# Fourteen expert tiles loaded into the ring before and beside the query weights, and priority for the choice of experts

## The chip, the cores and the metric

The kernel runs on one core of a Trainium2 chip. A core has five engines that run side by side and meet at semaphores: TensorE (PE in the profile), VectorE (DVE), ScalarE (ACT), GpSimd (POOL) and SyncE (SP). Sixteen DMA engines move data between HBM and the core's memory; here SP issues the plain loads and POOL issues the gathers of single rows. The metric is device time in microseconds (us) of one execution, the median of several.

## What is computed

One decoder block on 256 tokens of width 1024, all in float32: a state-space mixer beside causal attention, a gated merge, then an expert layer and a gated embedding. The change lies in the expert layer:

```python
def peer_ffn(h, w_q, keys1, keys2, u_tab, v_tab):
    q = (h @ w_q).reshape(B, S, 8, 2, 128)
    s1 = einsum('bshd,hnd->bshn', q[..., 0, :], keys1)   # 8 heads x 128 scores
    s2 = einsum('bshd,hnd->bshn', q[..., 1, :], keys2)
    v1, i1 = top_k(s1, 16);  v2, i2 = top_k(s2, 16)
    top, flat = top_k(v1[:, None] + v2[None, :], 16)     # 16 of 16 x 16 sums
    experts = e1 * 128 + e2                              # of 16,384 experts
    act = gelu(einsum('td,thkd->thk', h, u_tab[experts]))
    return einsum('thk,thkd->td', softmax(top) * act, v_tab[experts])
```

## The kernel before, in words

The kernel has two phases. Phase 1 (mixer, attention, merge) streams its weights in pieces of 512 KB through nine slots of a pool, `stream`; its pieces are asked for seven ahead of their use, `pssm` and `wout` among the last. The query weights `wq` come after them through the same slots. Phase 2 is the expert layer.

**The two halves of the tokens are treated differently.** For the first 128 tokens the products with *all* 16,384 experts are computed: the table `u` is read as 128 tiles of 512 KB, four tiles make a group (`s_group(g)`, 16 matmuls into `sp`, line 786), and the table `v` follows as 128 tiles. For the second 128 tokens only the chosen rows are fetched: `dot_rows(j)` gathers 128 rows of `u` (one row for each of 128 tokens) by an indirect DMA (line 750) and forms the dot products on VectorE (line 796); `v_chosen` does the like for `v`.

**The ring.** All of these tiles, `u` and `v` tiles (`dn`, issued by SP at line 745) and gathered rows (`sel`, issued by POOL), share one ring of `RING = 14` slots of 512 KB. A slot is given out in the order in which the program asks for it: the 15th asker waits until the first one's reader is done. Before the change the program asks in the order of use, four `u` tiles of a group, then two or three rows, then four `u` tiles:

```python
for g in range(GRP // 2):
    s_group(g)
    rows_until(g)          # rows up to (g + 1) * 88 // 32
    if g < 8:
        for i in (2 * g, 2 * g + 1):
            best(0, i, sc0[:, i, :])
    elif g < 10:
        choose(0, g - 8)
    elif g == 10:
        turn_choices(0)
```

**What must come before the rows.** The scores are made list by list: `lists(i)`, 16 of them, takes the piece `wq[i]`, splits it in two (ScalarE at line 116, POOL at line 120), multiplies (lines 144 to 147), turns the result into scores (line 840), copies them (lines 842 and 843; the copy `sc1` of the second half of the tokens has three buffers) and lets VectorE pick the 16 best (`best`, lines 824 to 828). After lists 0 to 7 `choose(1, 0)` combines them, on VectorE, into the row numbers `rowU` of the first 64 gathers (line 914); after lists 8 to 15 `choose(1, 1)` does the rest. `choose(0, 0)` and `choose(0, 1)` do the same later for the first 128 tokens, and `turn_choices(0)` then transposes their result on TensorE (line 929).

**What sets the order.** A scheduler in the compiler orders each engine's instructions ahead of time: of those that its own timing takes to be ready, it issues the one that the program names first, and a block under `tc.high_priority()` ranks ahead of the rest. Each engine then runs its list in that order. Matmuls under `in_turn()` stay in the order in which they are written.

Of the kernel before, what the change touches and what calls it, by code (L numbers as in the profile page):

```python
# [60 lines left out]
NS_POOL = 9  # L61
PLAN2 = "abr0c1d23"
RING = 14
GRP = NE // 4
DOTS_BY = 40
ROWS_FROM = 46
# [14 lines left out]
def block_kernel(ctx, tc, xT_d, xn_d, small_d, pos_d, pT_d, w_in_d, glu_d, pssm_d, patt_d, wout_d, wq_d,  # L81
# [32 lines left out]
    def split(src, hi, lo, pool_cols=None):  # L114

        nc.scalar.activation(hi, src, AF.Copy)  # L116
        n = src.shape[-1]
        pc = n if pool_cols is None else pool_cols
        if pc > 0:
            nc.gpsimd.tensor_tensor(lo[:, :pc], src[:, :pc], hi.bitcast(F32)[:, :pc], ALU.subtract)  # L120
        if pc < n:
            nc.vector.tensor_tensor(lo[:, pc:], src[:, pc:], hi.bitcast(F32)[:, pc:], ALU.subtract)

    def fetch(src_d):
        nat = stream.tile([P, PW], F32, name="nat", tag="w", bufs=WBUFS)
        nc.sync.dma_start(nat, src_d)
        return nat

    def piece(src_d, pool_cols=None, nat=None, at=None):
        if nat is None:  # L130
            nat = fetch(src_d)
        if at is None:
            hi = stream.tile([P, PW], F32R, name="whi", tag="w", bufs=WBUFS)
            lo = stream.tile([P, PW], F32R, name="wlo", tag="w", bufs=WBUFS)
        else:
            hi, lo = at
        split(nat, hi, lo, lo_cols[0] if pool_cols is None else pool_cols)
        return hi, lo

    def mm3(ps, pairs):  # L140

        n = len(pairs)
        for i, ((lh, ll), (rh, rl)) in enumerate(pairs):
            nc.tensor.matmul(ps, lh, rh, start=(i == 0), stop=False)  # L144
            nc.tensor.matmul(ps, lh, rl, start=False, stop=False)  # L145
        for i, ((lh, ll), (rh, rl)) in enumerate(pairs):
            nc.tensor.matmul(ps, ll, rh, start=False, stop=(i == n - 1))
# [96 lines left out]
    with ExitStack() as p1:  # L244
# [22 lines left out]
        def take():  # L267
            while len(ahead) < LEAD + 1 and todo:
                cut()
            return ahead.pop(0)  # L270
# [20 lines left out]
        w = D // SEG  # L291
# [344 lines left out]
        with tc.manual_schedule(engines={mybir.EngineType.PE}):  # L636
            for n, x in enumerate("u" * 4 + "q" * 4 + "k" * 4 + "v" * 4 + "z" * 16 + TAIL):
                while steps and steps[0][0] <= n:
                    steps.pop(0)[1]()
                i = counts.get(x, 0)  # L640
                counts[x] = i + 1
                pc = take()
# [13 lines left out]
        for i in range(4):  # L656
            pc = take()
# [7 lines left out]
        for c in range(DC):  # L665
            pc = take()
# [76 lines left out]
    def fetch_dense(src_d):  # L743
        nat = dense.tile([P, PW], F32, name="dn", tag="ring", bufs=RING)
        nc.sync.dma_start(nat, src_d)
        return nat

    def fetch_rows(src_d, rows):
        sel = dense.tile([P, D], F32, name="sel", tag="ring", bufs=RING)
        nc.gpsimd.indirect_dma_start(out=sel, out_offset=None, in_=src_d,  # L750
                                     in_offset=bass.IndirectOffsetOnAxis(ap=rows, axis=0))
        return sel
# [3 lines left out]
    def in_turn():  # L756
        return tc.issue_after(pe[0].ins) if pe[0] is not None else ExitStack()
# [7 lines left out]
        nc.scalar.activation(h1n[:, h * 512:(h + 1) * 512], ps, AF.Copy)  # L765

    turned_s = []

    def s_turn():

        g, sn = turned_s.pop(0)
        pt = psS.tile([P, 512], F32, name="pt", tag="T")
        with in_turn():
            for q in range(4):
                pe[0] = nc.tensor.transpose(pt[:, q * P:(q + 1) * P], sn[:, q * P:(q + 1) * P], ident)
        nc.scalar.activation(s_slots(g), pt.rearrange("p (q t) -> p q t", q=4), AF.Copy)

    def s_group(g):

        ps = psS.tile([P, 512], F32, name="sp", tag="S")  # L780
        for i in range(4):
            w = fetch_dense(u_d[4 * g + i]).rearrange("p (k n) -> p k n", k=2)
            with in_turn():
                for k in range(2):
                    c = 2 * i + k
                    pe[0] = nc.tensor.matmul(ps, hn[:, c, :P], w[:, k, :], start=(c == 0), stop=(c == DC - 1))  # L786
        sn = hx.tile([P, 512], F32, name="sn", bufs=2)
        nc.scalar.activation(sn, ps, AF.Gelu_apprx_tanh)  # L788
        if turned_s:
            s_turn()  # L790
        turned_s.append((g, sn))

    def dot_rows(j):

        sel = fetch_rows(urow_d, rowU[:, j:j + 1])
        nc.vector.scalar_tensor_tensor(sel, sel, 1.0, h1n, ALU.mult, ALU.mult, accum_out=dots[:, j:j + 1])  # L796

    with tc.tile_pool(name="topk", bufs=1, reuse_waits="tile") as tk:
# [21 lines left out]
        def best(t, i, sc):  # L820

            v1, ix = v1s[t], ixs[t]
            s2 = tk.tile([P, P], F32, name="s2", bufs=2)
            nc.vector.max(v1[:, i, 0:8], sc)
            nc.vector.match_replace(s2, v1[:, i, 0:8], sc, -3.0e38)
            nc.vector.max(v1[:, i, 8:16], s2)
            nc.vector.max_index(ix[:, i, 0:8], v1[:, i, 0:8], sc)
            nc.vector.max_index(ix[:, i, 8:16], v1[:, i, 8:16], s2)

        def lists(i):  # L830
            pc = piece(wq_d[i])
            ps = psS.tile([P, 512], F32, name="q2p", tag="S")
            with in_turn():
                hi, lo = (z.rearrange("p (k n) -> p k n", k=8) for z in pc)
                mm3(ps[:, :T], [((hi[:, k], lo[:, k]), (h2[0][:, k], h2[1][:, k])) for k in range(8)])
            q2 = tk.tile([P, T], F32, name="q2", bufs=2)
            nc.scalar.activation(q2, ps[:, :T], AF.Copy)
            px = psX.tile([P, 512], F32, name="scp", tag="X")
            for t in (1, 0):
                nc.tensor.matmul(px[:, t * P:(t + 1) * P], q2[:, t * P:(t + 1) * P], keys[:, i, :], start=True, stop=True)  # L840
            sc1 = tk.tile([P, P], F32, name="sc1", bufs=3)
            nc.scalar.activation(sc1, px[:, P:T], AF.Copy)
            nc.scalar.activation(sc0[:, i, :], px[:, :P], AF.Copy)
            best(1, i, sc1)
# [97 lines left out]
        for half in range(2):  # L942
            for i in range(8 * half, 8 * half + 8):
                lists(i)
            choose(1, half)
        nsel = 0

        def rows_until(g):
            nonlocal nsel
            while nsel < (g + 1) * (P - DOTS_BY) // GRP:  # L950
                dot_rows(nsel)
                nsel += 1

        for g in range(GRP // 2):
            s_group(g)
            rows_until(g)
# [7 lines that stand above are left out]
            elif g == 11:  # L964
                turn_choices(1)
# [59 lines left out]
    done = 0  # L1025
    for g in range(GRP // 2, GRP):
        s_group(g)
        rows_until(g)
        want = min(nb, (g + 1 - GRP // 2) * nb // (GRP // 2 - 1))
        while done < want:  # L1030
            g_step(done)
            done += 1
# [168 lines left out]
def layout(inputs):  # L1201
# [20 lines left out]
    def bmat(b):  # L1222
# [19 lines left out]
        "keys": k12.transpose(3, 0, 1, 2).reshape(P, 16, P),  # L1242
        "u": f["peer_u"][0].reshape(P, GRP, 4, 4, 2, P).transpose(1, 3, 5, 4, 2, 0).reshape(NE, P, PW),
        "urow": f["peer_u"][0],
# [23 lines left out]
```

## Time and profile before

| what | value |
|---|---|
| time, median of 3 runs | 1013.17 us (1012.89 to 1013.63) |
| the profiled execution's own time | 1015.38 us |
| its span, first to last instruction | 1013.6 us |
| busy share of the span: PE, DVE, ACT, POOL | 92%, 47%, 17%, 35% |
| mean DMA rate over the span | 312 GB/s |
| mean granted TensorE clock | 0.980 of full speed |

The spans of engines overlap, so their shares don't add up to 100%. The share of a whole span says little here: the two phases have different limits, and the stretch in which the change works, some 100 us around the start of phase 2, has to be read by itself.

### The profile page before, as it was taken

The page shows a single profiled execution, that of the slowest core. Times are in us where ns is not written, and L with a number is a line of the kernel's source. Part 1 is how long each engine was busy: PE and PEld are TensorE (multiplying, and loading weights), DVE is VectorE, ACT ScalarE, POOL GpSimd, SP SyncE. Part 2 cuts the span into 40 slices and gives each one's busy share as a digit, 9 for nine tenths or more (in the row PEclk, how much of TensorE's full clock was granted, in tenths as well). Part 3 has the DMA queues.
Part 4 walks back from the last instruction along what each step waited for, and adds up shares of the span by engine and source line. Part 5 has one row for each costly group of instructions (what it writes and reads, how often), then busy time and mean ns, then how long its engine had stood idle before and what let it go on. Part 6 is the DMA issues. An engine that isn't in the chain of part 4 may idle for free.

```text
span 1013.6 us, 10767 instructions
## 1 busy us (share of the span) xinstructions
PE 929.9 (92%) x3726; PEld 494.6 (49%) x3726; DVE 474.6 (47%) x1338; ACT 171.8 (17%) x356; POOL 350.7 (35%) x369
## 2 busy tenths in 40 slices
PE   7889999997999887999999988889997899999996
PEld 5446778885994333444554533334432333333332
DVE  5787781315498998445666766763100000000023
ACT  6523431014452130111111100000000000000013
POOL 2021020033555236333433445433443244444521
PEclk9999999998999998999999999999999899999998
DMA  9333235434358999999999999999999999999941
GB/s 351 128 104 104 83 103 194 160 98 142 129 205 332 409 407 375 409 410 409 409 409 410 409 409 409 410 408 395 407 409 411 384 410 409 410 409 410 406 171 42
DMA packets 87238, 316.65 MB, mean 312 GB/s; under 512 B 9856, under 2 KB 9872, under 8 KB 86672
## 3 DMA queue, kind: packets, MB, share of 16 engines
q1 hardware_dynamic: 49392, 178.54, 45.7%
q0 software_dynamic: 36928, 134.26, 33.5%
q10 hardware_dynamic: 864, 3.16, 0.9%
q8 instruction: 29, 0.48, 0.2%
q14 instruction: 25, 0.20, 0.1%
HBM read 313.83 MB, written 2.10 MB: 312 GB/s over the span
## 4 chain that ended last, share of the span: by engine, by line
PE 53%; DMA 27%; DVE 14%; issue 2%; ACT 2%; POOL 1%; POOLq 0%; DVEq 0%; SPq 0%; ACTq 0%
DMA dn<-in_v 12%; PE sp L786 10%; PE va L1062 10%; DMA sel<-in_v,rowV 8%; DMA dn<-in_u 7%; PE va L1072 6%; PE zp L153 5%; DVE sel L796 3%; PE nat L489 3%; PE wop L153 3%; PE gp L1162 2%; PE psp L153 1%; PE pap L153 1%; PE q2p L144 1%; PE q2p L145 1%
## 5 line engine op out<-in xcount | busy, mean ns | idle before, releaser
L786 PE MATMUL sp<-dn,hn 128*128 128x512 f32 x512 | 233.7, 602 | 11.0 <-DMA dn<-in_u 10.3
L750 POOL DMA_INDIRECT sel<-in_urow,rowU x128 | 150.1, 1172 | 214.3 <-PE sp L786 81.2
L750 POOL DMA_INDIRECT sel<-in_v,rowV x128 | 121.2, 947 | 179.6 <-PE va L1072 134.3
L796 DVE SCALAR_TENSOR_TENSOR sel<-sel,h1n 128x1024 f32<-128x1024 f32 x128 | 153.1, 1222 | 28.5 <-DMA sel<-in_urow,rowU 19.0
L786 PEld LDWEIGHTS sp<-dn,hn 128*128 128x128 f32 x512 | 93.4, 191 | 128.2 <-issue 91.7
L1062 PE MATMUL va<-dn,SA 128*128 128x512 f32 x256 | 123.5, 612 | 16.7 <-DMA dn<-in_v 16.7
L1062 PE MATMUL va<-dn,SB 128*128 128x512 f32 x256 | 118.1, 611 | 11.2 <-DMA dn<-in_v 11.2
L1072 PE MATMUL va<-sel,C 128*32 128x512 f32 x512 | 105.1, 598 | 6.0 <-DMA sel<-in_v,rowV 5.9
L1049 DVE TENSOR_TENSOR x_n<-x_n,va 128x512 f32<-128x512 f32 x4 | 2.6, 682 | 215.0 <-PE va L1072 215.0
L1062 PEld LDWEIGHTS va<-dn,SB 128*128 128x128 f32 x256 | 47.8, 193 | 81.6 <-issue 69.0
L1062 PEld LDWEIGHTS va<-dn,SA 128*128 128x128 f32 x256 | 44.6, 190 | 84.7 <-DMA dn<-in_v 43.8
L997 DVE TENSOR_TENSOR ohl<-oq,gTl 128x512 f16<-128x512 f16 x32 | 13.6, 425 | 117.0 <-PE gps L1011 60.3
L1072 PEld LDWEIGHTS va<-sel,C 128*32 128x32 f32 x512 | 26.8, 109 | 76.6 <-issue 55.3
L153 PE MATMUL zp<-hT,nat 128*128 128x256 f32 x256 | 58.0, 382 | 0.5 <-DVE gat L586 0.5
L788 ACT ACTIVATE sn<-sp 128x512 f32<-128x512 f32 x32 | 19.2, 599 | 210.8 <-PE sp L786 204.4
L1116 ACT ACTIVATE junk<-x_n 128x512 f32<-128x512 f32 x8 | 5.0, 629 | 278.2 <-PE va L1072 273.2
L153 PEld LDWEIGHTS zp<-hT,nat 128*128 128x128 f32 x256 | 47.7, 190 | 8.3 <-DVE gat L586 0.9
L120 POOL TENSOR_TENSOR wlo<-nat,whi 128x1024 fp32r<-128x1024 f32 x16 | 38.6, 2412 | 35.6 <-ACT whi L116 17.9
L453 POOL TENSOR_TENSOR wc<-wc,ws 128x512 f32<-128x512 f32 x8 | 10.3, 1293 | 110.3 <-DVE ws L452 102.4
L489 PE MATMUL nat<-nat,hT 128*128 128x512 f32 x96 | 45.9, 632 | 2.8 <-ACT qk L494 2.8
L144 PE MATMUL q2p<-hhi,whi 128*128 128x256 f32 x128 | 33.5, 297 | 5.4 <-ACT x_n L709 5.4
L1011 PE MATMUL gps<-ohh,o 128*128 128x64 f16 x256 | 35.5, 242 | 0.0
(293 smaller groups left out, 1130.2 us busy)
## 6 DMA issues: line engine op xcount, KB each, us to landing
dn<-in_u SPq DMA_DIRECT2D x128, 512.0 KB
dn<-in_v SPq DMA_DIRECT2D x128, 512.0 KB
nat<-in_w_in SPq DMA_DIRECT2D x31, 512.0 KB
nat<-in_wq SPq DMA_DIRECT2D x16, 512.0 KB
nat<-in_wout SPq DMA_DIRECT2D x8, 512.0 KB
g<-in_gate SPq DMA_DIRECT2D x8, 512.0 KB
nat<-in_patt SPq DMA_DIRECT2D x4, 512.0 KB
nat<-in_pssm SPq DMA_DIRECT2D x4, 512.0 KB
```

The costliest lines, as they stand in the source:

```text
L120: nc.gpsimd.tensor_tensor(lo[:, :pc], src[:, :pc], hi.bitcast(F32)[:, :pc], ALU.subtract)
L144: nc.tensor.matmul(ps, lh, rh, start=(i == 0), stop=False)
L153: nc.tensor.matmul(ps[:, :T], w[:, k, j * P:(j + 1) * P], a[:, k, :], start=(k == 0), stop=(k == kc - 1))
L489: nc.tensor.matmul(acc[t], hT[:, c, ts], pc[:, k, :], start=(c == 0), stop=(c == DC - 1))
L750: nc.gpsimd.indirect_dma_start(out=sel, out_offset=None, in_=src_d, in_offset=bass.IndirectOffsetOnAxis(ap=rows, axis=0))
L786: pe[0] = nc.tensor.matmul(ps, hn[:, c, :P], w[:, k, :], start=(c == 0), stop=(c == DC - 1))
L788: nc.scalar.activation(sn, ps, AF.Gelu_apprx_tanh)
L796: nc.vector.scalar_tensor_tensor(sel, sel, 1.0, h1n, ALU.mult, ALU.mult, accum_out=dots[:, j:j + 1])
L1011: pe[0] = nc.tensor.matmul(pv[:, i, :], o1[:, gi, :, ti], oh[:, gi, :, ti], start=False, stop=True)
L1062: pe[0] = nc.tensor.matmul(acc[0][d], s_slot(e2), nat[:, d * 512:(d + 1) * 512], start=(e2 == 0), stop=(e2 == NE - 1))
L1072: pe[0] = nc.tensor.matmul(acc[1][d][32 * q:32 * q + 32, :], C3[:, 32 * t:32 * t + 32], rows[q][:, d * 512:(d + 1) * 512], start=(s == 0), ...
L1162: pe[0] = nc.tensor.matmul(ps, hf[:, c, ts], w[:, c % 2, :], start=(c == 0), stop=(c == DC - 1))
```

## The change

`fetch_early` asks for ring slots for `u` tiles, and SP's loads into them, at an earlier place of the program: four tiles (`EARLY`) after the first three `wq` pieces, and one more in each of the next lists, until all 14 slots are asked for. `s_group` takes these tiles first. The pieces of `wq` are asked for three lists ahead of their use. The two calls of `choose(1, half)` stand under `tc.high_priority()`.

```diff
+EARLY = 4
...
+    early = []
+
+    def fetch_early(n):
+
+        while n and len(early) < RING:
+            early.append(fetch_dense(u_d[len(early)]))
+            n -= 1
...
-            w = fetch_dense(u_d[4 * g + i]).rearrange("p (k n) -> p k n", k=2)
+            w = (early.pop(0) if early else fetch_dense(u_d[4 * g + i])).rearrange("p (k n) -> p k n", k=2)
...
+        wq = [fetch(wq_d[i]) for i in range(3)]
+        fetch_early(EARLY)
+
         def lists(i):
-            pc = piece(wq_d[i])
+            pc = piece(None, nat=wq.pop(0))
+            if i + 3 < 16:
+                wq.append(fetch(wq_d[i + 3]))
+            fetch_early(1)
...
-            choose(1, half)
+            with tc.high_priority():
+                choose(1, half)
```

## Rows read from the trace of the kernel before

**Rows 1.** The page: busy time of the engines, and what the DMA engines moved in GB/s, in 40 slices of the span (25.3 us each).

```profile
PE 929.9 (92%) x3726; PEld 494.6 (49%) x3726; DVE 474.6 (47%) x1338; ACT 171.8 (17%) x356; POOL 350.7 (35%) x369
GB/s 351 128 104 104 83 103 194 160 98 142 129 205 332 409 407 375 409 410 409 409 409 410 409 409 409 410 408 395 407 409 411 384 410 409 410 409 410 406 171 42
```

**Rows 2.** The page's list of DMA issues: what is loaded, by which queue, how often, and how much each.

```profile
dn<-in_u SPq DMA_DIRECT2D x128, 512.0 KB
```

**Rows 3.** Stretches of the span: its ends and length; busy time (instructions) of PE, PEld, DVE, ACT and POOL; granted TensorE clock; busy share of the DMA engines; GB/s.

```profile
250.00:300.00 50.00, 50.00 (x413) 50.00 (x413) 31.94 (x173) 25.00 (x57) 27.50 (x12) 0.97 0.50 179
300.00:305.00 5.00, 5.00 (x33) 4.04 (x32) 5.00 (x20) 2.34 (x6) 1.49 (x1) 1.00 0.06 23
305.00:310.00 5.00, 5.00 (x13) 2.13 (x13) 4.93 (x28) 0.21 (x1) 1.07 (x1) 1.00 0.67 215
310.00:315.00 5.00, 5.00 (x19) 2.84 (x18) 2.55 (x14) 0.98 (x2) 3.78 (x4) 1.00 0.94 315
315.00:320.00 5.00, 5.00 (x19) 2.56 (x18) 4.46 (x9) 1.43 (x4) 4.02 (x4) 1.00 1.00 379
320.00:330.00 10.00, 10.00 (x28) 4.68 (x27) 10.00 (x57) 2.37 (x3) 5.45 (x5) 1.00 1.03 410
330.00:380.00 50.00, 43.52 (x112) 17.77 (x110) 49.90 (x250) 13.70 (x20) 13.89 (x14) 1.00 1.03 408
380.00:400.00 20.00, 13.62 (x35) 6.87 (x36) 19.59 (x48) 1.08 (x2) 11.34 (x8) 0.83 0.97 367
400.00:700.00 300.00, 277.33 (x1053) 132.72 (x1052) 178.73 (x335) 24.89 (x46) 122.31 (x104) 1.00 1.03 409
```

**Rows 4.** The chain of work that ended last, from 300 to 460 us: start, us, engine or DMA and what it made.

```profile
308.70 1.07 POOL sel L750
310.07 5.90 DMA sel<-in_urow,rowU
316.00 1.23 DVE sel L796 x2
...
380.32 1.15 DVE sel L796 x2
...
387.71 7.79 PE sp L786 x16
...
417.85 6.88 PE sp L786 x16
424.75 16.20 DMA dn<-in_u
```

**Rows 5.** SP's DMA issues in order of time, 150 to 300 us: start of the first, us from the first to the last, what is loaded, count.

```profile
163.81 2.69 SPq L745 DMA_DIRECT2D dn<-in_u  x4
168.81 3.78 SPq L126 DMA_DIRECT2D nat<-in_pssm  x2
...
210.25 81.24 SPq L126 DMA_DIRECT2D nat<-in_wq  x16
291.55 2.42 SPq L745 DMA_DIRECT2D dn<-in_u  x5
```

**Rows 6.** What SP's queue waited for between 291 and 330 us: line and releaser, us in total, times, the longest.

```profile
SPq L745 <- PE sp L786: 18.3, 6, 11.0
```

**Rows 7.** VectorE in order of time, 307 to 323 us: start, us, line and operation, count, in brackets the idle time before and what ended it.

```profile
308.19 0.23 DVE L914 SCALAR_TENSOR_TENSOR rowU<-dd 128x64 int32<-128x64 f16 x1
...
311.79 0.28 DVE L828 FIND_INDEX8 ix<-v,s 128x8 uint32<-128x128 f32 x1
314.50 1.23 DVE L796 SCALAR_TENSOR_TENSOR sel<-sel,h1n 128x1024 f32<-128x1024 f32 x1 [2.42 <-DMA sel<-in_urow,rowU]
...
316.00 1.23 DVE L796 SCALAR_TENSOR_TENSOR sel<-sel,h1n 128x1024 f32<-128x1024 f32 x1 [0.27 <-DMA sel<-in_urow,rowU]
...
318.74 1.23 DVE L796 SCALAR_TENSOR_TENSOR sel<-sel,h1n 128x1024 f32<-128x1024 f32 x1 [0.23 <-issue]
...
322.54 0.18 DVE L870 TENSOR_TENSOR cv<-v 128x32 f32<-128x32 f32 x1
```

**Rows 8.** GpSimd in order of time, 277 to 330 us, with the same columns.

```profile
282.50 2.42 POOL L120 TENSOR_TENSOR wlo<-nat,whi 128x1024 fp32r<-128x1024 f32 x1 [0.94 <-ACT whi L116]
...
310.07 0.95 POOL L750 DMA_INDIRECT sel<-in_urow,rowU  x1 [0.30 <-issue]
```

**Rows 9.** VectorE at 282 us, with the same columns.

```profile
282.56 2.41 DVE L870 TENSOR_TENSOR cv<-v 128x32 f32<-128x32 f32 x1
```

**Rows 10.** TensorE in order of time, 297 to 345 us, with the same columns.

```profile
303.11 7.03 PE L786 MATMUL sp<-dn,hn 128*128 128x512 f32 x16
309.58 1.52 PE L147 MATMUL q2p<-hhi,wlo 128*128 128x256 f32 x8
...
318.24 0.61 PE L840 MATMUL scp<-keys,q 128*128 128x128 f32 x4
...
331.80 1.98 PE L786 MATMUL sp<-dn,hn 128*128 128x512 f32 x4 [0.49 <-DMA dn<-in_u]
```

**Rows 11.** TensorE in order of time, 374 to 396 us, with the same columns.

```profile
386.38 0.69 PE L929 MATMUL tkT<-ident,en 128*128 128x128 f32 x2 [7.52 <-DVE en L915]
```

**Rows 12.** ScalarE in order of time, 290 to 304 us, with the same columns.

```profile
294.31 0.28 ACT L842 ACTIVATE sc<-scp 128x128 f32<-128x128 f32 x1
...
303.46 0.28 ACT L842 ACTIVATE sc<-scp 128x128 f32<-128x128 f32 x1 [2.07 <-DVE ix L827]
```

## The prediction, made before the changed kernel was run

> **What bounds the kernel now.** The page comes first, and in it the line of GB/s, not the busy shares: TensorE's 92% is a mean over stages with different limits [rows 1]. From the 14th slice to the 38th the DMA engines move 375 to 411 GB/s, and 400 to 700 us, taken alone, shows 409 at a DMA share of 1.03 [rows 1, 3]. So 409 GB/s is the rate of a full DMA here, a tile of 512 KB costs 524,288 B / 409 GB/s = 1.28 us [rows 2, 3], and from about 320 us on the kernel is as long as its tiles. Before 300 us the DMA engines are half idle (179 GB/s from 250 to 300). Whoever loads a tile there that is now loaded later saves up to 1.28 us, if nothing else is late.
>
> The second view is therefore the stretches around the switch. From 300 to 320 us the rate climbs from 23 over 215 and 315 to 379 GB/s, and at 380 to 400 us it sinks to 367 [rows 3]. The latter costs 20 us x (409 - 367) / 409 = 2.1 us of DMA time. These are the places where the DMA engines lose time that the change could give back.
>
> Third, the chain of waits tells who sets the end there. It does not run through the loads of `u`. It runs from the first gather (308.70) through its DMA (5.90 us) into VectorE's dot products and stays on VectorE to 380 us, then on TensorE from 387.71 to 424.73 without a gap, and only at 424.75 goes over to a load of `u` [rows 4]. VectorE is busy 49.90 of 50.00 us from 330 to 380 [rows 3]. TensorE at 386.38 had stood 7.52 us waiting for `en`, the last result of `choose(0, 1)` [rows 11]: its transposes are in its queue ahead of the next `u` group, the ring stays full behind them, and this is the dip to 367 GB/s. So what the changed stretch is worth is read from VectorE, not from the ring alone.
>
> Fourth, VectorE in order of time between 307 and 323 us: `rowU` is written at 308.19, the lists' work ends at 312.07, and then VectorE stands 2.42 us for the first gathered rows, and 0.27 and 0.23 us for two later ones [rows 7]: 2.92 us idle in a stretch whose length VectorE sets. It has nothing else to do there because list 15's scores leave TensorE only at 318.24, behind the first two `u` groups [rows 10], so `choose(1, 1)` can't begin.
>
> **The change, part by part.**
>
> *Fourteen u tiles early.* Before, SP issues four at 163.81 and five at 291.55, all ahead of the first group at 303.11 [rows 5, 10]; the tenth waits for a slot, 11.0 us long, until that group frees one [rows 6]. After, 14 can lie there: five more, 5 x 1.28 = 6.4 us of DMA time at most. Not all of it lasts. All 14 slots then hold `u` tiles, and each next transfer, the first gathers too, waits until TensorE has read a tile: one per 1.88 us (four groups with their transposes take the 30.1 us from 387.71 to 417.85, so a group of four tiles 7.5 us [rows 4]). Count tiles at 330 us. Before: 9, then from 305 to 320 (215 + 315 + 379) x 5 us = 4.5 MB = 8.7 tiles, then 410 x 10 us = 7.8 tiles: 25.5 [rows 3]. After: 14, then (330 - 305) / 1.88 = 13.3, of which up to one is still on its way: 26.3 to 27.3. The lead has shrunk from 5 tiles to 0.8 to 1.8; I take 1.5, or 1.9 us. The bounds are 0 (the lead is eaten) and 6.4 us (kept whole).
>
> *What hides the moved loads.* Ten more loads now stand before or among the `wq` pieces on SP's queue, 12.8 us of DMA time. I cost them at nothing: the DMA engines move 179 of 409 GB/s between 250 and 300, and TensorE, which uses the pieces, is busy 50.00 of 50.00 us there [rows 3]. A `wq` piece with a `u` tile beside it takes 2.6 us, against 81.24 us / 16 = 5.1 us from one `wq` issue to the next [rows 5]. If they go out right behind the four at 163.81, the `pssm` pieces at 168.81 are behind them, with the `wout` ones after; these are asked for seven pieces ahead. With that cover gone, one list would be late once, by 1.28 us.
>
> *wq three lists ahead.* It adds no instruction. It can bring list 15's weights to TensorE ahead of the first `u` group; its last eight matmuls, 1.52 us [rows 10], then come before that group instead of behind it, which costs TensorE nothing over the three groups.
>
> *Priority for the choosing.* No instruction is added. `choose(1, 0)` already stands in the program ahead of lists 8 to 15, so the new rank alone can't let it pass much; where its steps wait on one another other work still fills in. For `choose(1, 1)` it means: as soon as list 15 is there, ahead of the dot products. Nothing needs its result before the 65th gather, but it is work that VectorE can do while the rows are on their way. The gap of 2.42 us and the two small ones are then filled, whichever comes first, list 15 or the rows. The price is between 0 (the gap remains) and -2.92 us; I take -2.92, since either of the two changes is enough. The dot products behind `choose(1, 1)` don't hold up the ring at once: the first gathered row's slot is next wanted 14 requests later, by the 18th `u` tile, and TensorE has not read the 14th before 303.1 + 14 x 1.88 = 329 us.
>
> *A rule that speaks against it.* A 128x32 sum of `choose(1, 0)` took 2.41 us at 282.56, and the same line took 0.18 us at 322.54; the first lay under a POOL split from 282.50 to 284.92 [rows 7 to 9]. By that, choosing beside the splits costs up to 2.2 us for each it meets, before and after alike, and I add nothing. The Trainium skill (SBUF — State Buffer, section SBUF: two separate sides) says that GpSimd and a VectorE instruction with two inputs in SBUF share a port pair as an exclusive lock, so that the loser stands for the whole instruction. The trace agrees with it, 2.41 against 2.42 us. By it alone, `choose(1, 0)` could not become faster while lists are still split, and `rowU` would stay near 308: the first rival.
>
> **The sum.** On VectorE's chain -2.92 us. Can the DMA follow? It has the lead of 1.9 us and the 2.1 us lost at 380 to 400, together 4.0 us, so the chain is the smaller of the two and decides. Everything from `choose(0, 1)` on comes 2.9 us earlier, and from 424 us on the full DMA carries it unchanged to the end. The profiled execution took 1015.38 us, its span of 1013.6 and 1.8 around it: after, 1012.5. The median of the runs lies 2.2 below that execution: 1013.17 - 2.9 = 1010.3 us.
>
> **The rivals.**
>
> *No change, 1013.2 us.* VectorE's gap stays. For it: each gather now needs a freed slot, one every 1.88 us, against 1.25 us from one to the next when slots are free (310.07, 0.95 and 0.30 idle [rows 8]), so rows reach VectorE more thinly; `rowU` may stay at 308; list 15 may stay behind the `u` groups. Against it: with `wq` asked for earlier the last reason goes. Chance 0.30.
>
> *More, about 1007 us.* TensorE's stand of 7.52 us [rows 11] shrinks too, because `choose(0, 1)` ends before TensorE's queue comes to its transposes. Then the DMA's account holds alone: 4.0 us, 1009.2, and with the whole lead of five tiles 6.4 + 2.1 = 8.5 us, 1004.7. Against it: VectorE has no other idle time to give. Chance 0.11.
>
> *Slower, about 1017 us.* With its rank `choose(1, 0)` holds VectorE in one piece. From 282.56 to 308.19 it shares 25.6 us with the lists [rows 7, 9]; half of that, 12.8 us, is its own by my estimate. The scores have three buffers, and three lists take 9.15 us (294.31 to 303.46 [rows 12]); past that point ScalarE stands at the copy of scores, and TensorE's lists behind it, for 12.8 - 9.15 = 3.7 us. TensorE's `u` groups then begin that much later, with the ring full and the DMA idle: 1013.2 + 3.7 = 1016.9. For it: ScalarE already waited 2.07 us for VectorE at 303.46 [rows 12]. Against it: the work that fills in is ready, the choosing's next step mostly not. Chance 0.15.
>
> **How the numbers follow.** The forecast, VectorE's gaps closed, has the remaining chance of 0.44 and lies between 1008.5 and 1012. A difference of 0.2%, 2 us, is about what a measurement of this kernel can tell from none. A small part of the forecast's case, 0.04, stays within it, so faster 0.51, same 0.34, slower 0.15. The range takes in the no-change case and reaches into the two outer ones: 1006 to 1015.5.
>
> **What would show it.** In the changed profile: SP's issues with 14 `u` loads ahead of 303 us; rates near 280 GB/s (524 KB / 1.88 us) from 305 to 329, lower than before, then 409; no gap over 1 us on VectorE between 307 and 320; list 15's scores before 312; TensorE's stand for `en` ending near 383.5. Wrong I would be if VectorE's first dot product again follows a wait of 2 us or more, if ScalarE's score copies wait over 3 us for VectorE between 288 and 303, or if the stand at `en` is gone altogether.

## The result, and the profile of the changed kernel

The changed kernel takes 1020.53 us (median of 22 runs, 1015.8 to 1028.12) where the kernel before, run beside it, takes 1013.4 (1011.24 to 1020.88). The ratio is 1.0062, 95% interval 1.0043 to 1.0081: slower by 0.6%, some 7 us, where 1010.3 and a range of 1006.0 to 1015.5 were forecast.

The profiled execution is one of the slow ones of its spread: 1026.38 us, span 1024.6. Of the 11.0 us to the profiled execution of before, 4.0 arise before the lists begin, where TensorE ran at its lower level for longer: the mean clock of the first 166 us is 0.96, before 0.98, and until there both programs have the same instructions. So everything below is counted from the lists' first matmul, which serves for the other kernels too. From it to the end of the span it is 772.1 us, before 765.1: 7.0 us more, as in the medians.

TensorE in order of time, the lists' first matmul, in the kernel before:

```profile
248.51 0.58 PE L144 MATMUL q2p<-hhi,whi 128*128 128x256 f32 x1 [5.43 <-ACT x_n L709]
```

The changed kernel's page, busy time and GB/s in 40 slices (25.6 us each), for [rows 1]:

```profile
PE 939.0 (92%) x3726; PEld 499.4 (49%) x3726; DVE 477.6 (47%) x1338; ACT 170.7 (17%) x356; POOL 347.1 (34%) x369
GB/s 349 136 92 121 65 90 248 318 120 138 128 80 172 411 408 308 386 410 409 408 409 409 409 408 409 410 408 409 409 409 410 387 409 409 410 409 409 409 183 41
```

The busy times hardly differ. The GB/s do: in the 13th slice 172 where before had 332, and in the 16th and 17th 308 and 386 where before had 375 and 409. Four stretches at the same distance from the lists' first matmul (50, 60, 80, 140 and 170 us behind it) narrow it down, the kernel before first; columns as in [rows 3]:

```profile
298.50:308.50 10.00, 10.00 (x54) 7.09 (x53) 9.97 (x47) 3.08 (x7) 2.39 (x1) 1.00 0.40 139
308.50:328.50 20.00, 20.00 (x62) 9.97 (x61) 16.97 (x79) 4.78 (x9) 14.00 (x13) 1.00 0.98 370
328.50:388.50 60.00, 47.14 (x122) 20.08 (x121) 59.52 (x277) 13.70 (x20) 16.51 (x16) 0.95 1.01 401
388.50:418.50 30.00, 30.00 (x82) 14.03 (x81) 18.75 (x42) 4.25 (x8) 18.14 (x12) 0.98 1.01 394
```

The changed kernel:

```profile
302.50:312.50 10.00, 10.00 (x78) 10.00 (x78) 10.00 (x45) 2.20 (x9) 2.33 (x1) 0.89 0.00 1
312.50:332.50 20.00, 20.00 (x60) 9.88 (x60) 15.46 (x71) 4.13 (x9) 11.89 (x10) 1.00 0.65 210
332.50:392.50 60.00, 53.39 (x138) 22.36 (x136) 56.99 (x279) 15.96 (x23) 20.18 (x19) 1.00 1.03 409
392.50:422.50 30.00, 21.29 (x53) 10.34 (x54) 24.29 (x47) 2.17 (x4) 13.77 (x10) 0.77 0.81 303
```

In tiles of 512 KB this is (139 - 1) x 10 us = 2.6 tiles lost, (370 - 210) x 20 us = 6.1 lost, 0.9 won, and (394 - 303) x 30 us = 5.2 lost. It came to the 50 us mark 6.4 tiles ahead; at 170 us it is 6.7 behind, and stays there: 8.6 us of a full DMA, of which the end gives some back. There are two places to explain.

*First place: the lists end late.* SP's issues, for [rows 5], show all 14 `u` loads by 179 us:

```profile
166.20 4.85 SPq L746 DMA_DIRECT2D dn<-in_u  x8
171.21 0.63 SPq L127 DMA_DIRECT2D nat<-in_pssm  x1
172.41 6.76 SPq L746 DMA_DIRECT2D dn<-in_u  x6
...
212.65 77.95 SPq L127 DMA_DIRECT2D nat<-in_wq  x16
326.59 6.93 SPq L746 DMA_DIRECT2D dn<-in_u  x4
```

Then the ring is full until the first `u` group reads a tile. ScalarE in order of time, for [rows 12], the kernel before first:

```profile
291.31 0.26 ACT L919 ACTIVATE gate<-gate 128x64 f32<-128x64 f32 x1 [1.06 <-DVE gate L918]
```

```profile
295.02 1.28 ACT L934 ACT_TABLE_LOAD   x1
300.85 0.26 ACT L934 ACTIVATE gate<-gate 128x64 f32<-128x64 f32 x1 [4.55 <-DVE gate L933]
301.01 0.37 ACT L852 ACTIVATE q<-q2p 128x256 f32<-128x256 f32 x1
```

And TensorE, for [rows 10, 11]:

```profile
252.47 0.58 PE L145 MATMUL q2p<-hhi,whi 128*128 128x256 f32 x1 [5.32 <-ACT x_n L710]
...
301.43 1.22 PE L855 MATMUL scp<-keys,q 128*128 128x128 f32 x4 [3.63 <-ACT q L852]
...
313.37 7.03 PE L795 MATMUL sp<-dn,hn 128*128 128x512 f32 x16
320.24 0.61 PE L855 MATMUL scp<-keys,q 128*128 128x128 f32 x4
...
401.21 0.69 PE L944 MATMUL tkT<-ident,en 128*128 128x128 f32 x2 [10.57 <-DVE en L930]
```

The `Exp` of the gate of `choose(1, 0)` stands in ScalarE's list in front of the `q` copy of list 11. VectorE has not made its operand; ScalarE stands 4.55 us (in the kernel before 1.06, at 291.31), the finished list waits for its copy, TensorE stands 3.63 us for that `q`. The granted clock then is at the lower level, half of full speed, for 3.4 us (most of it in the first stretch, hence its 0.89). The first `u` group starts 60.9 us after the lists' first matmul; before, 54.6.

Why is VectorE late? GpSimd and VectorE in order of time (in the first VectorE line, one of the seven sums takes 1.97 us of the 2.46):

```profile
286.09 2.40 POOL L121 TENSOR_TENSOR wlo<-nat,whi 128x1024 fp32r<-128x1024 f32 x1 [0.49 <-ACT whi L117]
289.85 2.39 POOL L121 TENSOR_TENSOR wlo<-nat,whi 128x1024 fp32r<-128x1024 f32 x1 [1.37 <-ACT whi L117]
292.73 4.80 POOL L121 TENSOR_TENSOR wlo<-nat,whi 128x1024 fp32r<-128x1024 f32 x2 [0.49 <-ACT whi L117]
```

```profile
286.56 2.46 DVE L889 TENSOR_TENSOR cv<-v 128x32 f32<-128x32 f32 x7
290.41 1.90 DVE L889 TENSOR_TENSOR cv<-v 128x64 f32<-128x64 f32 x1
293.63 1.62 DVE L875 CAST ixf<-ix 128x128 f32<-128x128 uint32 x1
296.39 1.16 DVE L877 CAST dx<-ixf 128x8 f16<-128x8 f32 x1
...
314.65 0.20 DVE L929 SCALAR_TENSOR_TENSOR rowU<-dd 128x64 int32<-128x64 f16 x1
...
320.23 1.23 DVE L805 SCALAR_TENSOR_TENSOR sel<-sel,h1n 128x1024 f32<-128x1024 f32 x1 [3.22 <-DMA sel<-in_urow,rowU]
```

With `wq` three ahead the splits come closer together, and four of them, two back to back, fall between the first candidate sum of `choose(1, 0)` and the gate's subtraction; before, two. Each time VectorE has an instruction that takes until the split is over or up to 0.14 us longer. Added up over the instructions that took over 0.15 us more than the median of their line and operation, this is 5.9 us ahead of the gate and 1.7 between it and `rowU`; in the kernel before, 2.2 and 5.4. The sum is the same, 7.6, but it has moved in front of the result for which ScalarE waits here. Ten more instructions of the lists' maxima lie there too (70 VectorE instructions in all, against 60). This is read from the traces; no run moves the splits alone.

*Second place: the stand for `en`.* 10.57 us ending at 401.21, before 7.52 [rows 11]; the clock is low (0.77 over the fourth stretch), and DMA moves 303 GB/s. The growth has a cause of its own. VectorE and GpSimd in the changed kernel, and VectorE in the kernel before:

```profile
397.81 3.35 DVE L930 CAST en<-dd 128x128 f32<-128x128 f16 x1
```

```profile
397.55 3.53 POOL L987 MEMSET C<- 128x4096 f32 x1
```

```profile
386.10 0.23 DVE L915 CAST en<-dd 128x128 f32<-128x128 f16 x1
```

The cast that writes the last `en` took 3.35 us and ended 0.08 us after a GpSimd memset that had begun 0.26 us before it; in the kernel before, where that memset begins at 391.10, the same cast took 0.23. By the trace it is the delay seen at the splits, now with a memset, and its 3.1 us are the whole growth of the stand (10.57 - 7.52). Of all kernels here only the changed one and `e1` below have it, both with `wq` ahead and the early tiles; in the others no cast of `en` takes over 0.37 us. DMA keeps its rate for most of the stand, 405, 411 and 379 GB/s in the three slices of 5 us from 387 us. Then it stops, and SP waits up to 14.9 us for TensorE to read a tile (370 to 412 us):

```profile
402.00:407.00 5.00, 5.00 (x9) 2.36 (x8) 4.81 (x15) 0.00 (x0) 0.15 (x1) 0.50 0.08 28
```

```profile
SPq L746 <- PE sp L795: 18.0, 4, 14.9
```

### The profile page after: what moved, and what is told of

Its sections match the earlier page's. It is cut to its first block, busy times and chain, and to the rows that moved or that the text cites. A ratio compares the mean times of both kernels' runs of the same rounds, so it can differ in the third digit from the quotient of the medians.

```text
span 1024.6 us, 10783 instructions
## 1 busy us (share of the span) xinstructions
PE 939.0 (92%) x3726; PEld 499.4 (49%) x3726; DVE 477.6 (47%) x1338; ACT 170.7 (17%) x356; POOL 347.1 (34%) x369
## 4 chain that ended last, share of the span: by engine, by line
PE 48%; DMA 33%; DVE 12%; issue 3%; ACT 2%; POOL 2%; SPq 0%; POOLq 0%; ACTq 0%
DMA dn<-in_v 13%; DMA dn<-in_u 11%; PE va L1078 9%; DMA sel<-in_v,rowV 7%; PE sp L795 7%; PE va L1088 6%; PE zp L154 5%; PE wop L154 3%; PE nat L490 3%; PE gp L1178 2%; DVE sel L805 2%; DMA sel<-in_urow,rowU 2%; PE psp L154 1%; PE pap L154 1%; PE q2p L145 1%
## 5 line engine op out<-in xcount | busy, mean ns | idle before, releaser
L751 POOL DMA_INDIRECT sel<-in_urow,rowU x128 | 146.7, 1146 | 226.9 <-PE sp L795 81.7
L1088 PE MATMUL va<-sel,C 128*32 128x512 f32 x512 | 107.6, 598 | 5.0 <-DMA sel<-in_v,rowV 5.0
L154 PE MATMUL zp<-hT,nat 128*128 128x256 f32 x256 | 60.2, 392 | 0.5 <-DVE gat L587 0.5
```

The lines of the kernel that those rows point to most:

```text
L154: nc.tensor.matmul(ps[:, :T], w[:, k, j * P:(j + 1) * P], a[:, k, :], start=(k == 0), stop=(k == kc - 1))
L1088: pe[0] = nc.tensor.matmul(acc[1][d][32 * q:32 * q + 32, :], C3[:, 32 * t:32 * t + 32], rows[q][:, d * 512:(d + 1) * 512], start=(s == 0), ...
```

## The experiments

Tiles of 512 KB that DMA has moved, against the kernel before at the same time after the lists' first matmul (worked out from the sizes of the DMA records of each profiled execution; 0.78 tile is 1 us of a full DMA; the column `before` is that kernel's own count):

```
 us  before  changed  no prio.  wq only  u only  wq,Exp late  changed,  changed,
                       (e1)     (f1)     (f2)    (g3)         en late   both late
                                                              (m1)      (m3)
 50   85.8    +6.4     +6.4     +1.4     +6.4    +1.4         +6.4      +6.4
 60   88.5    +3.7     +3.7     -1.3     +3.8    -0.3         +3.7      +3.8
 80  102.6    -2.4     -1.3     -3.3     -0.1    -0.6         -2.3      -0.9
100  118.1    -2.3     -1.4     -3.3     -0.0    -1.1         -2.2      -0.9
110  125.9    -2.3     -1.3     -6.1     +0.0    -2.3         -2.1      -0.8
140  148.5    -1.5     -1.2     -6.2     -0.8    -4.7         -1.3      -0.9
170  171.0    -6.7     -5.6     -7.8     -1.2    -6.2         -0.5      -0.0
500  427.6    -6.0     -4.8     -7.0     -0.5    -6.3         -1.5      -1.8
```

From the lists' first matmul to the end of the span, the same executions take, in the order of the columns, 765.1, 772.1, 770.2, 772.7, 764.1, 770.7, 765.0 and 765.1 us. Two programs below that equal the kernel before take 763.6 and 764.1, so some 1.5 us between single executions say nothing.

**The three edits one by one.** `e1` is the changed kernel without the priority block:

```
-            with tc.high_priority():
-                choose(1, half)
+            choose(1, half)
```

> The changed kernel without the priority: ring filled early and wq three ahead stay, choose is issued as before. Three theories. A, the order: loading wq three ahead lets the lists' work stand earlier in the order in which the instructions are written to the engines, so that choose(1,0) lies one list later on VectorE (rowU behind list 13's maxima instead of list 12's) and ScalarE's Exp of the gate stands in front of a list's q copy with its operand still unmade; this edit alone carries the loss: about 1020 us (+6 to +7 on the kernel before), and the first u group starts 60 to 62 us after the lists' first matmul, as in the changed kernel (60.9), where the kernel before needs 54.6. B, the priority: it is what puts choose's instructions, and with them the Exp, ahead of the lists' copies; without it the time falls back to 1011 to 1013.5 us and the lists to about 55 us. C, the ring: 14 u tiles leave the gathered rows no slots, and DMA stands idle until the u groups free some; the loss stays, about 1020 us, but with the lists at 55 us and the loss behind the first u group.

Measured: 1018.65 us, ratio 1.0039 (1.0015 to 1.0063), an interval that overlaps the changed kernel's; the first `u` group 59.8 us after the lists' first matmul. `e2` adds only the priority block to the kernel before:

> The kernel before with choose(1, half) in the priority block and nothing else. A (order from the weights' loads): the written order hardly moves, so 1013 us, within 2 us of the kernel before, first u group 54 to 56 us after the lists' first matmul. B (priority): the whole loss, about 1020 us, ScalarE standing at the Exp for 4 to 5 us and TensorE at the next q for 3 to 4 us. C (ring): 1013 us.

Measured: 1015.09 us, ratio 1.0021 (0.9998 to 1.0043), first `u` group at 54.7, ScalarE's wait at the `Exp` 1.1 us. `f1` keeps of the change only this:

```
+        wq = [fetch(wq_d[i]) for i in range(3)]
...
-            pc = piece(wq_d[i])
+            pc = piece(None, nat=wq.pop(0))
+            if i + 3 < 16:
+                wq.append(fetch(wq_d[i + 3]))
```

> Of the change only the loads of wq three pieces ahead; no early u tiles, no priority. A (order): the whole loss, 1018 to 1021 us, first u group 60 to 62 us after the lists' first matmul, ScalarE at the Exp for 4 to 5 us. B (priority): 1013 us. C (ring): 1013 us, lists at 55 us, because the u tiles are loaded as in the kernel before.

Measured: 1021.2 us, ratio 1.0063 (1.0043 to 1.0084), first `u` group at 60.0. What was waited for in its lists (275 to 313 us: engine, line and releaser; us in total, times, the longest):

```profile
ACT gate L932 <- DVE gate L931: 3.4, 1, 3.4
PE scp L853 <- ACT q L850: 2.5, 1, 2.5
```

`f2` keeps of the change only `fetch_early` and its use in `s_group`; each `wq` piece is loaded where it is split.

> Of the change only the 14 early u tiles; each wq piece is loaded where it is split, as before, and there is no priority. A (order): lists at 54 to 56 us, and what is left is the worth of the five more tiles, 0 to 2 us: 1011 to 1013.5 us. B (priority): the same, about 1013 us or less. C (ring): the loss, 1017 to 1020 us, with DMA at rest before the first u group and rows waiting for slots; lists at 55 us.

Measured: 1015.65 us, ratio 1.0014 (0.9991 to 1.0036), first `u` group at 54.5. So loading `wq` three ahead carries a loss of the full size, though not by the same way: by the table `f1` is 6.1 tiles behind at 110 us, ahead of its stand for `en`, and loses 1.7 more by 170; the changed kernel is 2.3 behind at 110 and loses 4.4 more by 170. B falls: without the priority the lists are as late, and the priority adds about 1 us to the `Exp`'s wait (3.4 without, 4.55 with). C falls as the cause: with 14 early tiles and an empty DMA (rest from 295 to 311 us) nothing is lost. But nothing is won either: the 6.4 tiles of lead at 50 us are gone at 80.

**Is it the `Exp`?** `f1` once more, with the gate parts of `choose(1, 0)` and `choose(1, 1)` (the subtraction on VectorE, the `Exp` and what follows it) written behind both, and the first `Exp` queued behind list 13's score copy:

```
+            with tc.issue_after(copied[13].ins):
+                nc.scalar.activation(gx, gx, AF.Exp)
```

> The kernel with only wq loaded three ahead (1021.2 us, first u group 60.0 us after the lists' first matmul), with one thing more: the gate's Exp of choose(1,0) stands on ScalarE behind the score copies of list 13 and no longer ahead of the q copies of lists 11 and 12; the gate's tv gets a second buffer for it. Loads, splits, VectorE's order of choose(1,0) stay. Theory A, the Exp at the head of ScalarE's queue: in that run it waited 3.4 us for VectorE, TensorE then 2.5 us for the q copy, and its clock was at the lower level for 3.4 us behind that; without it the lists take 55 to 56.5 us and the time is 1014 to 1017 us. Rival A2, the layout as a whole (two q copies and two splits in a row, scores one list later): the wait only moves to another copy, the lists stay at 59 to 60 us and the time at 1019 to 1021 us.

Measured: 1020.51 us, ratio 1.008 (1.0051 to 1.0109); first `u` group at 55.6. Half of it came as A said, the lists are back to within 1.0 us of the kernel before; the time is not. The table shows why: it is 0.6 tiles behind at 80 us and 6.2 at 170. What is won at the lists is lost again between 100 and 170 us, where two more stands lie. ScalarE and TensorE in this run:

```profile
349.22 0.26 ACT L939 ACTIVATE gate<-gate 128x64 f32<-128x64 f32 x1 [16.22 <-DVE gate L937]
349.50 1.28 ACT L797 ACT_TABLE_LOAD   x1
350.79 0.60 ACT L797 ACTIVATE sn<-sp 128x512 f32<-128x512 f32 x1
```

```profile
351.44 1.11 PE L784 MATMUL pt<-ident,sn 128*128 128x128 f32 x4 [5.12 <-ACT sn L797]
...
380.62 0.69 PE L949 MATMUL tkT<-ident,en 128*128 128x128 f32 x2 [12.08 <-DVE en L930]
```

The third `Exp`, that of `choose(0, 0)`, stands 16.22 us in front of a Gelu, and TensorE 5.12 us for the tile that this Gelu makes; then comes the stand for `en`. Theory A was too narrow: each result of the choosing that VectorE owes to the head of another engine's list can be such a place. These two stands are not the whole of it: without them (`n1`, below) 3.9 of the 6.2 tiles are still lost.

**Programs that turned out the same.** Three kernels were meant to test sizes and the stand for `en`:

> wq loaded one piece ahead instead of three, no early u tiles, no priority. In this program ScalarE's and VectorE's orders through the lists are those of the kernel before (Exp between the score copies of lists 9 and 10, rowU behind list 12's maxima), only the loads are issued earlier. Theory A (the loads hurt only through the order that they lead to): lists 54 to 56 us, 1012.5 to 1015 us. Rival D (earlier loads or their splits as such take VectorE's or DMA's time): 57 us and more, 1016 to 1019 us.

> The kernel before, with turn_choices(0) and (1) at u groups 13 and 14 instead of 10 and 11, and nothing of the change. In the kernel before TensorE stands 7.5 us there for en of choose(0,1), its clock is at the lower level for 6.8 us after, and DMA moves 333, 398, 368 and 370 GB/s in the four slices of 5 us from 380 us, where it has 409 before and after: 2.1 us of transfers. If this stand is on the path, 1010.5 to 1012 us; if the ring's 14 tiles cover it, 1013 to 1014 us; if the later rowV holds back the second table's rows, slower, 1016 us or more.

> The 14 early u tiles alone (1015.65 us, lists 54.5 us) with turn_choices at u groups 13 and 14. In the run with early tiles alone the transfers that were 5.2 tiles ahead at 300 us were 0.5 ahead at 325 us, and TensorE stood for en at 394 us. If the stand is what took the rest: 1011 to 1013 us, below the kernel before by 1 to 2 us. If the early tiles are worth nothing because the ring is full before the first u group: the same as the kernel before with the late turn alone.

Measured: 1013.43 us (0.9996, 0.9968 to 1.0023), 1013.17 (1.0011, 0.9989 to 1.0034) and 1015.82 (1.0024, 0.9999 to 1.0048). But all five engines' lists are, instruction by instruction, those of the kernel before in the first two, and those of `f2` in the third: the later call left the transposes where they were, and one piece ahead is what SP's list had already. They test no theory. They show instead what the measurement does on equal programs (0.9996 and 1.0011), and give `f2` a second result: the early tiles alone are worth nothing, or cost up to 0.5%.

**The stand for `en`, truly moved.** The changed kernel with the transposes of `turn_choices` in TensorE's written order, and called at groups 13 and 14:

```
-            elif g == 10:
+            elif g == 13:
                 turn_choices(0)
...
-            for e in range(2):
-                nc.tensor.transpose(ps[:, e * P:(e + 1) * P], ens[t][:, e, :], ident)
+            with in_turn():
+                for e in range(2):
+                    pe[0] = nc.tensor.transpose(ps[:, e * P:(e + 1) * P], ens[t][:, e, :], ident)
...
```

> The changed kernel with the transposes of turn_choices put behind the matmuls of u groups 13 and 14 on TensorE, by the same ordering that the u groups use among themselves; nothing else. In the profile of the changed kernel the transfers, counted in tiles of 512 KB from the lists' first matmul, fall from 0.7 tiles behind the kernel before at 145 us to 6.7 behind at 170 us, around TensorE's 10.57 us stand for en of choose(0,1). Theory E (that stand, on TensorE, is what costs these tiles, because the u tiles behind it keep their slots): the tiles are kept, 1014 to 1017 us. Rival F (VectorE is late with its dot products there, and the gathered rows keep the slots): the fall stays, 1019 to 1021 us.

Measured: 1016.2 us, ratio 1.0022 (1.0001 to 1.0044). Theory E holds, F does not: the table keeps the tiles from 140 to 170 us (-1.3 to -0.5, where the changed kernel falls from -1.5 to -6.7). The same stretch, 140 to 170 us, and TensorE:

```profile
389.30:419.30 30.00, 25.89 (x67) 10.45 (x66) 19.61 (x35) 4.25 (x8) 13.26 (x11) 1.00 1.03 410
```

```profile
390.28 7.74 PE L795 MATMUL sp<-dn,hn 128*128 128x512 f32 x16
397.85 0.60 PE L784 MATMUL pt<-ident,sn 128*128 128x128 f32 x4
398.29 3.78 PE L795 MATMUL sp<-dn,hn 128*128 128x512 f32 x8
...
428.06 0.38 PE L945 MATMUL tkT<-ident,en 128*128 128x128 f32 x2
```

410 GB/s instead of 303, the clock at 1.00 instead of 0.77, and no wait in front of the transposes. The lists in this run are as late as in the changed kernel (first `u` group at 60.9), and still it ends level with the kernel before (765.0 against 765.1 us): late lists alone cost this kernel nothing that its profiled execution shows. The cast of `en` takes its usual time here (at most 0.37 us), since the memset too comes later, at 434 us. So the run shows what the whole stand costs, and not which part of it the memset's 3.1 us are; no run moves the memset alone.

**Both kinds of stand taken away**, in the changed kernel, in the kernel before, and with the early tiles alone. The `Exp`s are queued as in `g3`, the other three behind the Gelus of groups 6, 10 and 12:

> The kernel of the run before this one with the four Exps of the gates put later on ScalarE as well: behind list 13's score copy, and behind the Gelus of u groups 6, 10 and 12. Theory A plus E (ScalarE at an Exp whose operand VectorE has not made holds back first the lists and then the turned s tiles, and TensorE behind them): lists 55 to 57 us, no PE wait for a Gelu between the lists and 180 us after their first matmul; 1009 to 1013 us, so that what is left of the change is no loss. Rival F (VectorE's total of choose and dot products sets the pace, and every wait taken away comes back as a wait for the rows' slots): 1016 to 1020 us.

> The kernel before with the same two things (Exps later, transposes of turn_choices behind u groups 13 and 14), nothing of the change. The kernel before loses 1.6 tiles of transfers between 130 and 160 us after the lists' first matmul, around its 7.5 us stand. Theory A plus E: 1010 to 1012 us. Rival F: 1013 us.

> As the run before, with the 14 early u tiles as well (wq loaded where it is split). If the early tiles are worth the 0.5 tile that they kept at 330 us: 0.6 us less than that run; if they cost by putting four more dot products ahead of list 15 and choose(1,1) on VectorE: 1 to 3 us more.

Measured: 1015.68 us (1.0011, 0.9989 to 1.0033), 1014.52 (1.0004, 0.9983 to 1.0024), 1016.38 (1.001, 0.9989 to 1.0032). For the changed kernel the mechanism is as expected (first `u` group at 55.6, in the table level with the kernel before at 170 us): its loss can no longer be told from none. But against `m1` the `Exp`s bring no more than 0.5 us by medians and nothing by the profiled executions (765.0 and 765.1). That it would then win was wrong: expected were 1009 to 1013. And none of these versions beats the kernel before: without its own stand that kernel is 0.5 tile better off at 160 us than at 130 (0.3 behind, then 0.2 ahead of its profiled execution), where 1.6 were expected. The early tiles on top again bring nothing (1.9 us more by medians, the intervals overlap).

**The rest with `wq` ahead alone.** `f1` with both kinds of stand removed, and with the one for `en` only:

> Only wq three ahead, with the four Exps of the gates put later on ScalarE (behind list 13's score copy and the Gelus of u groups 6, 10 and 12) and turn_choices' transposes behind u groups 13 and 14. If the loss of wq ahead (1021.2 us) is made of nothing but the stands that it leads to: lists 55 to 56 us, no more than 1 tile behind the kernel before at 170 us after the lists' first matmul, 1012 to 1015 us. If the earlier loads cost time by themselves: 1017 us and more.

> Only wq three ahead, with turn_choices' transposes behind u groups 13 and 14; the Exps stay. With wq ahead alone the tiles fell behind in three places: 3.3 tiles by 80 us after the lists' first matmul, 2.8 between 100 and 110 us (there ScalarE waited 15.40 us at an Exp with a Gelu behind it, and TensorE 2.96 us for that Gelu), and 1.7 between 130 and 160 us (the stand for en). If each stand is a loss of its own, only the last is saved: 1018 to 1020 us. If the ring makes good what was lost before, as in the changed kernel without its stand (3.3 tiles fewer behind at 170 than at 80): 1014 to 1016 us.

Measured: 1018.78 us (1.0058, 1.0034 to 1.0082) and 1019.11 (1.0046, 1.0027 to 1.0064). The second came as the first of its readings said. The first missed: without the two kinds of stand 3.9 tiles are lost at 170 us (6.2 in `g3`, 7.8 in `f1`), 1.6 of them between 100 and 110 us. In that run, two stretches, what SP waits for (325 to 362 us), and TensorE:

```profile
345.00:350.00 5.00, 5.00 (x16) 2.47 (x15) 5.00 (x29) 1.09 (x2) 4.39 (x3) 1.00 0.82 262
350.00:355.00 5.00, 1.57 (x3) 0.50 (x2) 5.00 (x24) 0.00 (x0) 0.92 (x2) 0.88 0.95 327
```

```profile
SPq L746 <- DVE sel L806: 15.3, 2, 9.3
```

```profile
354.17 6.92 PE L796 MATMUL sp<-dn,hn 128*128 128x512 f32 x12 [3.43 <-DMA dn<-in_u]
```

VectorE is busy without a gap, a gathered row keeps its slot until its dot product comes, SP's next `u` load waits 9.3 us for that slot, and TensorE 3.43 us for the load. So read, it is rival F after all, in the kernel without early tiles, for half of what `f1` loses. In the changed kernel it doesn't show (-2.3 at 100, -2.3 at 110 us). Why 14 early tiles keep it away was not tested.

## Why the prediction was wrong, point by point

**DMA sets the pace from about 320 us on: right.** 409 GB/s in both outside the dips, and what is lost at 170 us is, to within 2 tiles, what is lost at 500 (changed -6.7 and -6.0, `m3` 0.0 and -1.8).

**Fourteen early tiles: loaded as foretold, but worth nothing.** 14 issues stand ahead of 303 us. With the lists on time (`f2`) the lead at 330 us of that run is 0.5 tile (104.2 against 103.7 in all), and this is what the lists' start, 0.66 us earlier in that execution, gives by itself; at 80 us after their first matmul it is -0.1. Taken was 1.5, and 0 was the bound. In the changed kernel the lead shrank from 6.4 to 3.7 tiles before the first `u` group started, and was gone at 80 us.

**Moved loads hidden: right.** In `f2` the lists take 54.5 us as before.

**`wq` three ahead "adds no instruction" and costs nothing: the step that failed.** `f1` alone costs 0.63%, 7.8 tiles at 170 us. It changed no amount of work, but the order of it in the engines' lists, the place of the `Exp` and the gate among them. The prediction asked what the loads do to the DMA and to TensorE, and never in which order the engines would then be given their work. What that order costs is shown for the changed kernel: the stand for `en` (`m1`). In `f1` the stands explain half of the tiles (`n1`: 3.9 are still lost without them); the rest is read as VectorE's dot products holding the rows' slots, and its cause stays open.

**The rule on the shared port: applied to the sum, not to the place.** The prediction found the lock in the trace, 2.41 beside 2.42 us [rows 8, 9], and dropped it as equal before and after. Its sum is: 7.6 us in both. Its place is not: 5.9 instead of 2.2 us ahead of the gate, and 3.1 us more at the cast of `en`, beside a memset that the prediction did not look at. The Trainium skill (SBUF — State Buffer, section SBUF: two separate sides) says the loser of the lock stands for the other's whole instruction, and names besides VectorE instructions with two inputs those in a mode that takes both ports; the casts of 1.16 and 1.62 us beside the splits agree, a cast of `dx` else taking 0.15, though no run shows in which mode they went. Whether a delay matters is seen from who waits for the delayed instruction.

**Priority fills VectorE's gap, -2.92: wrong.** The gap grew: 3.22 us before the first dot product, where before had 2.42 [rows 7]. "Either of the two changes is enough" was the error: list 15's scores still stand behind the first `u` group (320.24), so that no rank could bring `choose(1, 1)` forward. The priority alone (`e2`) leaves ScalarE's and TensorE's lists as they were, and moves the time not measurably (1.0021, 0.9998 to 1.0043).

**The stand for `en`, foretold to end near 383.5: wrong.** It ended at 401.21 and grew to 10.57 us, by the 3.1 us of the delayed cast. Without it (`m1`) 4.3 us of the 7.1 are gone by medians of two series (1020.53 to 1016.2), and all of them by the profiled executions (772.1 to 765.0 from the lists' first matmul on). The chain of waits had shown it at 7.52 us, and the prediction used it only as a rival's gain.

**The rival that came nearest is the slower one**, 1016.9 with a chance of 0.15: `u` groups 3.7 us late, ring full, DMA idle. Measured are 6.3 us late and DMA at 1 GB/s. But the nearness is luck, for its cause was not the one named: ScalarE stood at a single `Exp`, not at the score copies; and its account ended at the lists, whose lateness by itself shows no cost in `m1`'s profiled execution, while the loss was taken at the stand that followed. Of the three signs of a wrong prediction one came, the first dot product behind a wait of over 2 us, and one nearly: ScalarE stood over 3 us for VectorE, but at the `Exp`.

The account in the end, by medians of separate series: 7.1 us over the kernel before, 4.3 of it at the stand for `en` (`m1`), 0.5 more with the `Exp`s moved (`m3`), and 2.3 that two medians of this spread can't tell from nothing.

## What to carry to other kernels

That a load adds no instruction does not make it free to issue earlier: where a scheduler lays out the engines' lists by estimated readiness, an earlier load moves other instructions, so compare the lists of the two programs engine by engine before reading times. Look for a small instruction on whose result another engine's list stands, and for what delays it: here a 0.26 us `Exp` ahead of TensorE's copies, and a cast of 0.23 us that took 3.35 beside a memset. Then ask whether the wait reaches the end: the first stand hardly did, the second did once the ring was full. And a lead in a ring whose slots are full by the time that the reader starts is worth only what the reader's start leaves of it; here 6.4 tiles became none in 30 us.

## What was unexpected of the hardware

TensorE's clock made the stands dearer: it was at the lower level (1.2 GHz) for 3.4 us right behind 3.63 us without work, and for 13.7 us, from 393.4 to 407.1, within and behind the 10.57 us; there eight matmuls of a `u` group took 5.96 us instead of 3.60. Executions of one and the same program differ by up to 11 us (kernel before, 35 runs of one series: 1010.54 to 1021.63). The profiled ones differ, ahead of anything that the change touches, in how long the clock is at the lower level: 13.7 us of the first 166 in the changed kernel's, 6.8 in the kernel before's. What brings this about stays open.
